# The attention layer of a four-layer latent backbone: another form of its scores, softmax division and value products

## The chip, the cores and the metric

The kernel runs on one core of a Trainium2 chip. The time is that of one launch in device microseconds; the median of several runs counts, and for the kernel before there are three: 2109.61, 2110.99 and 2111.64 us. The profile is that of one further execution.

## The reference

A block of four layers with mixers A, B, C, A, each followed by an MLP, on 256 latent and 256 context tokens of width 1024, in fp32. The change lies in mixer B, layer 1: attention of 16 query heads of 64 columns on 4 key heads, with a learned sink logit for each head. Latent queries see all context tokens and the latent tokens within 128 positions; context queries see context tokens alone.

```python
def sink_softmax(scores, sink):
    m = sink
    for s in scores:
        m = jnp.maximum(m, jnp.max(s, axis=-1))
    ps = [jnp.exp(s - m[..., None]) for s in scores]
    denom = jnp.exp(sink - m)
    for p in ps:
        denom = denom + jnp.sum(p, axis=-1)
    return [p / denom[..., None] for p in ps]

def swa_mixer(xc, xl, w_qkv, sinks, w_out, ang_row, ang_col, ctx_out):
    scale = B_HEAD_DIM ** -0.5
...
    mask = (jnp.abs(qpos - kpos) <= B_WINDOW) & (kpos >= 0) & (kpos < S)
    s_loc = jnp.einsum('bnqhgd,bnkhd->bnhgqk', qb, kb).astype(jnp.float32) * scale
    s_loc = jnp.where(mask[None, :, None, None], s_loc, -jnp.inf)
    s_ctx = jnp.einsum('bnqhgd,bchd->bnhgqc', qb, kc).astype(jnp.float32) * scale
    p_loc, p_ctx = sink_softmax([s_loc, s_ctx], sink[None, None, :, :, None])
    o_l = (jnp.einsum('bnhgqk,bnkhd->bnqhgd', p_loc.astype(vb.dtype), vb)
           + jnp.einsum('bnhgqc,bchd->bnqhgd', p_ctx.astype(vc.dtype), vc))
    yl = o_l.reshape(bn, S, D_MODEL) @ w_out
    if ctx_out:
        s_c = jnp.einsum('bqhgd,bkhd->bhgqk', qc, kc).astype(jnp.float32) * scale
        (p_c,) = sink_softmax([s_c], sink[None, :, :, None])
        o_c = jnp.einsum('bhgqk,bkhd->bqhgd', p_c.astype(vc.dtype), vc)
        yc = o_c.reshape(bn, xc.shape[1], D_MODEL) @ w_out
```

## The kernel before

Tokens lie along the free dimension: a tile `h[:, c, :]` holds 128 of the 1024 columns for 512 tokens, 0 to 255 latent and 256 to 511 context. Each weight block (128x1024 raw) is loaded by the queue of SP, cast to a high half on ScalarE (L241) and to the remaining low half on VectorE (L246). A product is the sum of three: high by high, high weight by low input, low weight by high input (`mm3`, L390 to L392). `w_get(ahead)` hands out the next block in a fixed list (`weight_order`) and has blocks split up to `ahead` further ones; four raw blocks and five pairs of halves are held.

The engines work off the instructions in the order in which the code issues them. So the order of calls in `mixer_b` is the schedule.

Mixer B first computes keys and ten blocks `u` of 128 columns (0 and 1 are keys, 2 to 9 queries), each with `chunk`: 24 products of 512 columns, after which `evac` splits the result into halves (`put`); the latent half is rotated first (`rotate`, and one TensorE product in `rest`). A query tile `Q2` holds the high half of one head's 64 columns on 64 partitions and the low half on the other 64, a key tile `K2` the high half of the keys on both. Then `v_step` computes values, and 32 units follow, a unit being 128 queries of two heads (`hh` 0 and 1) that share `G`, `blk` and `j`; `blk` 0 and 1 are latent queries on 512 keys, 2 and 3 context queries on 256. The order of blocks is 0, 2, 1, 3: four latent units, four context units, and so on, eight blocks in all. In step `x` of `attend`:

- `s1(x)` makes the scores of two heads in a bank each: one full-height product (high and low query halves by high keys, L1288), one of 64 rows for the low half of the keys (L1292), and for latent queries the window mask, added through an identity product of 256 columns (L1295).
- `s4(x-2)` transposes the exponentials (L1348), and ScalarE copies them out (L1350). `over_sum(x-2)` puts the reciprocal of each sum, as a diagonal matrix, through a product with ones (L1369), so that it lies in the layout of the result.
- `pv(x-3)` multiplies by the values, 128 query columns at a time (L1360).
- `s2(x)` takes on VectorE the maxima (L1309, L1314) and for unit `x-1` the sums' reciprocals and diagonals, and on ScalarE the exponentials with their sums (L1331).

After four units `block_end` multiplies the result by the reciprocals on VectorE (L1381); in the next step ScalarE casts it (L1338), and VectorE subtracts for the low half (L1339). The tile `h` is scratch during this and is saved to and restored from HBM. The output projection (`residual`, L565) follows: two of its eight blocks are begun among the last units, three follow as chunks, three go into `transition`, which also sums squares for the next normalisation (`stats_add`, L434) and takes their sum over partitions in a TensorE product (`stats_mm`, L465).

## Time and profile before

| | |
|---|---|
| median of three runs | 2110.99 us (2109.61 to 2111.64) |
| the profiled execution | 2114.74 us |
| its span on the core | 2113.0 us |
| TensorE busy | 2053.4 us (97%) |
| VectorE busy | 1453.5 us (69%) |
| ScalarE busy | 948.9 us (45%) |
| chain of waits, TensorE's share | 92% |

The span runs from the first instruction to the last; the launch takes somewhat longer. Shares are means over stages that differ. Matmuls are pipelined: the time from one start to the next tells their cost, not the length of a row.

### The profile page before, as it was taken

The page shows a single profiled execution, that of the slowest core. Times are in us where ns is not written, and L with a number is a line of the kernel's source. Part 1 is how long each engine was busy: PE and PEld are TensorE (multiplying, and loading weights), DVE is VectorE, ACT ScalarE, POOL GpSimd, SP SyncE. Part 2 cuts the span into 40 slices and gives each one's busy share as a digit, 9 for nine tenths or more (in the row PEclk, how much of TensorE's full clock was granted, in tenths as well). Part 3 has the DMA queues.
Part 4 walks back from the last instruction along what each step waited for, and adds up shares of the span by engine and source line. Part 5 has one row for each costly group of instructions (what it writes and reads, how often), then busy time and mean ns, then how long its engine had stood idle before and what let it go on. Part 6 is the DMA issues. An engine that isn't in the chain of part 4 may idle for free.

```text
span 2113.0 us, 30325 instructions
## 1 busy us (share of the span) xinstructions
PE 2053.4 (97%) x11730; PEld 1751.2 (83%) x11730; DVE 1453.5 (69%) x2652; ACT 948.9 (45%) x1814; POOL 87.0 (4%) x138
## 2 busy tenths in 40 slices
PE   6989999999999999999999999999999999989998
PEld 4767798888889878988888988898888899889997
DVE  5667777787777775677777764467777776576554
ACT  3436653324236685624333343262433435556554
POOL 0123100000000000000000000000000000310000
PEclk9999999999999999999999999999999999999999
DMA  9783245565553104266565433236556533635552
GB/s 300 272 264 103 64 135 179 177 193 185 184 170 119 50 2 138 92 189 189 179 194 175 130 112 98 94 108 189 187 180 197 179 122 104 175 103 180 184 185 91
DMA packets 97025, 326.11 MB, mean 154 GB/s; under 512 B 17760, under 2 KB 18928, under 8 KB 96240
## 3 DMA queue, kind: packets, MB, share of 16 engines
q1 hardware_dynamic: 81184, 293.81, 43.5%
q0 software_dynamic: 15152, 29.83, 4.6%
q8 instruction: 92, 1.51, 0.3%
q10 hardware_dynamic: 544, 0.52, 0.1%
q14 instruction: 53, 0.43, 0.1%
HBM read 319.73 MB, written 4.33 MB: 153 GB/s over the span
## 4 chain that ended last, share of the span: by engine, by line
PE 92%; DVE 3%; DMA 2%; ACT 2%; issue 1%; POOL 0%; SPq 0%; DVEq 0%; ACTq 0%
PE bank L390 25%; PE bank L392 25%; PE bank L391 25%; PE bank L591 2%; PE bank L592 2%; PE bank L594 2%; PE bank L422 1%; PE bank L1348 1%; PE bank L423 1%; PE bank L424 1%; PE bank L1360 1%; DMA ab<-dar 1%; PE bank L1288 1%; PE bank L1025 1%; DVE wlo L246 1%; PE bank L1000 1%
## 5 line engine op out<-in xcount | busy, mean ns | idle before, releaser
L390 PE MATMUL bank<-xh,whi 128*128 128x512 f32 (+1 forms) x1600 | 579.4, 362 | 1.7 <-ACT h L912 1.0
L241 ACT CAST whi<-raw 128x1024 fp32r<-128x1024 f32 x374 | 387.1, 1044 | 421.1 <-PE bank L391 382.8
L391 PE MATMUL bank<-xl,whi 128*128 128x512 f32 (+1 forms) x1600 | 574.4, 359 | 0.2
L392 PE MATMUL bank<-xh,wlo 128*128 128x512 f32 (+1 forms) x1600 | 573.9, 359 | 0.0
L246 DVE TENSOR_TENSOR wlo<-raw,whi 128x1024 fp32r<-128x1024 f32 x374 | 455.6, 1225 | 152.5 <-ACT whi L241 151.9
L353 DVE SCALAR_TENSOR_TENSOR junk<-ada,cbc 128x1024 bf16<-128x1024 f32 x320 | 390.7, 1221 | 18.1 <-DMA ada<-in_ada 13.8
L390 PE MATMUL bank<-hh,whi 128*128 128x512 f32 (+1 forms) x1096 | 384.5, 351 | 0.0
L392 PE MATMUL bank<-hh,wlo 128*128 128x512 f32 (+1 forms) x1096 | 383.9, 350 | 0.0
L391 PE MATMUL bank<-hl,whi 128*128 128x512 f32 (+1 forms) x1096 | 383.9, 350 | 0.0
L390 PEld LDWEIGHTS bank<-xh,whi 128*128 128x128 f32 x1600 | 304.9, 191 | 49.9 <-ACT h L912 1.6
L392 PEld LDWEIGHTS bank<-xh,wlo 128*128 128x128 f32 x1600 | 304.9, 191 | 44.3
L391 PEld LDWEIGHTS bank<-xl,whi 128*128 128x128 f32 x1600 | 305.0, 191 | 44.0 <-DVE xl L945 1.0
L391 PEld LDWEIGHTS bank<-hl,whi 128*128 128x128 f32 x1096 | 207.4, 189 | 27.4
L392 PEld LDWEIGHTS bank<-hh,wlo 128*128 128x128 f32 x1096 | 207.4, 189 | 27.2
L390 PEld LDWEIGHTS bank<-hh,whi 128*128 128x128 f32 x1096 | 207.4, 189 | 27.1
L565 DVE SCALAR_TENSOR_TENSOR h<-bank,mod,h 128x256 f32<-128x256 f32 x280 | 125.6, 479 | 133.1 <-PE bank L392 133.1
L676 DVE TENSOR_TENSOR hl<-q,hh 128x512 fp32r<-128x512 f32 (+1 forms) x137 | 81.5, 595 | 170.5 <-ACT q L675 170.2
L673 ACT ACTIVATE r<-bank 128x512 f32<-128x512 f32 (+1 forms) x137 | 70.8, 517 | 269.2 <-PE bank L392 266.2
L459 ACT ACTIVATE sq<-h 128x256 f32<-128x256 f32 (+1 forms) x74 | 36.0, 487 | 139.4 <-DVE h L565 114.2
L591 PE MATMUL bank<-xh,whi 128*128 128x256 f32 x312 | 81.4, 289 | 3.5 <-ACT xh L527 3.5
L592 PE MATMUL bank<-xh,wlo 128*128 128x256 f32 x312 | 80.2, 285 | 0.0
L674 ACT ACTIVATE hh<-r 128x512 fp32r<-128x512 f32 (+1 forms) x137 | 75.9, 554 | 4.6
(274 smaller groups left out, 2129.3 us busy)
## 6 DMA issues: line engine op xcount, KB each, us to landing
raw<-in_wts SPq DMA_DIRECT2D x374, 512.0 KB, 4.2
ada<-in_ada SPq DMA_DIRECT2D x160, 512.0 KB, 3.5
start<-in_ada SPq DMA_DIRECT2D x16, 512.0 KB, 9.1
first<-in_ada POOLq DMA_DIRECT2D x12, 512.0 KB, 6.0
cbc<-line POOLq DMA_DIRECT2D x4, 1024.0 KB, 7.8
rb<-dnm POOLq DMA_DIRECT2D x16, 256.0 KB, 7.1
ab<-dar POOLq DMA_DIRECT2D x16, 256.0 KB, 12.2
h<-in_hin SPq DMA_DIRECT2D x4, 512.0 KB, 6.8
```

Source lines behind the costliest of these rows:

```text
L241: self.nc.scalar.copy(hi, self.raw[j])
L246: self.nc.vector.tensor_tensor(out=lo, in0=self.raw.pop(j), in1=hi.bitcast(F32), op=ALU.subtract)
L353: nc.vector.scalar_tensor_tensor(out=junk, in0=w, scalar=1.0, in1=self.cbc[:, s, :], op0=ALU.mult, op1=ALU.mult, accum_out=self.mods[l][:, ...
L390: mm(out, lhsT=whi, rhs=xhi, start=first, stop=False)
L391: mm(out, lhsT=whi, rhs=xlo, start=False, stop=False)
L392: mm(out, lhsT=wlo, rhs=xhi, start=False, stop=last)
L565: self.nc.vector.scalar_tensor_tensor(out=self.h[:, m, a:b], in0=o[:, a - sl.start : b - sl.start], scalar=mod[:, gate + m, s : s + 1], in ...
L591: mm(o[:, :T], lhsT=w[0][:, c], rhs=hi[:, sl], start=(k == 0), stop=False)
L592: mm(o[:, :T], lhsT=w[1][:, c], rhs=hi[:, sl], start=False, stop=False)
L673: nc.scalar.activation(r[:, :n], o, AF.Relu)
L674: nc.scalar.activation(hh[:, sl], r[:, :n], AF.Square)
L676: nc.vector.tensor_tensor(out=hl[:, sl], in0=q[:, :n], in1=hh[:, sl].bitcast(F32), op=ALU.subtract)
```

## The change

The low half of the keys now fills both halves of its own tile for each key head (`KL[g]`), so its product takes the same 128-row query tile as the high half's; the mask product covers only the 128 columns that can be masked. `maxima` takes both heads of a unit in one VectorE instruction. The exponentials are multiplied by the reciprocal of their sum on VectorE before they are transposed (`normalise`), in place of the diagonal product and of the multiplication at the block's end. Two units (a pair `y`) go into one value product of 256 columns. Scores lie in banks 3, 4 and 6, 7, transposes in a ring of banks 0, 1, 2, results in bank 5; one in four of the copies of a latent pair is made on VectorE. The query blocks 8 and 9 come after the values (their weights too, in `weight_order`), the second of them among the first units, and five of the output projection's blocks are begun at the end; their second halves follow, each with the split of one weight block.

```diff
@@ weight_order
-            order += [("colq", "b_w_qkv", i, m) for m in range(8)]
+            order += [("colq", "b_w_qkv", i, m) for m in range(6)]
             order += [("mov", "b_w_qkv", i, 1280, 256, kk) for kk in range(2)]
+            order += [("colq", "b_w_qkv", i, m) for m in range(6, 8)]
@@ mixer_b
-            KL = [bp.tile([128, 512], F32R, name=f"KL{G}") for G in range(2)]
+            KL = [bp.tile([128, 512], F32R, name=f"KL{g}") for g in range(4)]
...
                     away = slice(64 - 64 * hh, 128 - 64 * hh)
                     if u < 2:
                         hi = K2[2 * u + hh]
-                        lo = KL[u][rows, sl]
+                        lo = KL[2 * u + hh]
                         nc.scalar.copy(hi[away, sl], src[rows])
+                        parts.append((rows, hi[rows, sl], lo[rows, sl]))
+                        parts.append((rows, hi[rows, sl], lo[away, sl]))
                     else:
                         hi = Q2[u - 2][hh]
-                        lo = hi[away, sl]
+                        parts.append((rows, hi[rows, sl], hi[away, sl]))
                     nc.scalar.activation(hi[rows, sl], src[rows], AF.Copy, scale=scale)
-                    parts.append((rows, hi[rows, sl], lo))
...
-                def rest():
-                    rp = self.aux()[:, 0:T]
+                def rest(bank=None):
+                    rp = (self.aux() if bank is None else bank)[:, 0:T]
...
-            for u in range(3, 10):
+            for u in range(3, 8):
             units = [(G, blk, j) for G in range(2) for blk in (0, 2, 1, 3) for j in range(4)]
...
+            N = len(units) // 2
+            bk = self.banks
+            tring, po = [bk[0], bk[1], bk[2]], bk[5]
+            S, P, sums = {}, {}, {}
...
-                ss = [ring[2 * (x % 2) + hh] for hh in range(2)]
+                at = 3 + 3 * (x % 2)
+                ss = self.allb[:, at : at + 2, 0:nk]
                 qs = Q2[G * 4 + j]
                 for hh in range(2):
-                    nc.tensor.matmul(ss[hh][:, :nk], lhsT=qs[hh][:, ts_], rhs=K2[2 * G + hh][:, k0:512], start=True, stop=False)
+                    g = 2 * G + hh
+                    nc.tensor.matmul(ss[:, hh, :], lhsT=qs[hh][:, ts_], rhs=K2[g][:, k0:512], start=True, stop=False)
+                    nc.tensor.matmul(ss[:, hh, :], lhsT=qs[hh][:, ts_], rhs=KL[g][:, k0:512], start=False, stop=not lat)
+                if lat:
+                    c = (1 - blk) * 128
+                    for hh in range(2):
+                        nc.tensor.matmul(
+                            ss[:, hh, c : c + 128], lhsT=self.ident16, rhs=self.mask_w[:, blk * T + c : blk * T + c + 128],
+                            start=False, stop=True,
+                        )
+                S[x] = ss
+            def maxima(x):
+                G, blk, j = units[x]
+                y, a = divmod(x, 2)
+                if a == 0:
+                    sums[y] = [bq.tile([128, 4], F32, tag=t, name=t, bufs=4) for t in ("ngm", "es", "rs")]
+                ngm = sums[y][0]
+                c = slice(2 * a, 2 * a + 2)
+                ci = G * 4 + j
+                nc.vector.tensor_reduce(ngm[:, c], S[x], axis=AX.X, op=ALU.max, negate=True)
+                nc.vector.tensor_tensor(out=ngm[:, c], in0=ngm[:, c], in1=self.nsinks[:, 2 * ci : 2 * ci + 2], op=ALU.min)
+                if a == 1:
+                    nc.vector.tensor_tensor(
+                        out=sums[y][1], in0=ngm, in1=self.nsinks[:, 2 * ci - 2 : 2 * ci + 2], op=ALU.subtract
+                    )
+            def exps(x):
+                y, a = divmod(x, 2)
+                ngm, es, rs = sums[y]
+                P[x] = []
                 for hh in range(2):
...
+                    p = bq.tile([128, 512], F32, tag="p", name="p", bufs=8)
+                    nk = S[x].shape[-1]
+                    at = 2 * a + hh
+                    nc.scalar.activation(
+                        p[:, :nk], S[x][:, hh, :], AF.Exp, bias=ngm[:, at : at + 1], accum_out=rs[:, at : at + 1]
+                    )
+                    P[x].append(p[:, :nk])
+                if a == 1:
+                    nc.scalar.activation(es, es, AF.Exp)
+            def normalise(y):
+                ngm, es, rs = sums.pop(y)
+                nc.vector.tensor_tensor(out=rs, in0=rs, in1=es, op=ALU.add)
+                nc.vector.reciprocal(rs, rs)
+                for a in range(2):
                     for hh in range(2):
...
+                        p = P[2 * y + a][hh]
+                        nc.vector.tensor_scalar(p, p, rs[:, 2 * a + hh : 2 * a + hh + 1], None, op0=ALU.mult)
+            def turn(x):
+                nk = len(keys_of(units[x][1])[0]) * 128
+                at = 2 * (x % 4)
+                ps = P.pop(x)
+                if nk == 512:
+                    for hh in range(2):
+                        tp = tring[tpos[0] % 3]
+                        tpos[0] += 1
+                        for c in range(0, nk, 128):
+                            nc.tensor.transpose(tp[:, c : c + 128], ps[hh][:, c : c + 128], self.ident)
+                        if hh * (x % 2):
+                            nc.vector.tensor_copy(self.h[:, at + hh, :], tp)
+                        else:
+                            nc.scalar.copy(self.h[:, at + hh, :], tp)
+                else:
+                    tp = tring[tpos[0] % 3].rearrange("p (a k) -> p a k", a=2)
+                    tpos[0] += 1
+                    for hh in range(2):
+                        for c in range(0, nk, 128):
+                            nc.tensor.transpose(tp[:, hh, c : c + 128], ps[hh][:, c : c + 128], self.ident)
+                    nc.scalar.copy(self.h[:, at : at + 2, 0:nk], tp)
+            def pv(y):
+                G, blk, j = units[2 * y]
-                js = slice(j * 128, j * 128 + 128)
+                at = 4 * (y % 2)
                 for c, kc in enumerate(kcs):
                     for hh in range(2):
                         g = 2 * G + hh
                         nc.tensor.matmul(
-                            po[64 * hh : 64 * hh + 64, js], lhsT=vv[:, kc, g * 64 : g * 64 + 64], rhs=PT[x][hh][:, c, :],
+                            po[64 * hh : 64 * hh + 64, j * 128 : j * 128 + 256], lhsT=vv[:, kc, g * 64 : g * 64 + 64],
+                            rhs=self.h[:, at + hh : at + hh + 3 : 2, c * 128 : c * 128 + 128],
                             start=(c == 0), stop=(c == len(kcs) - 1),
                         )
...
+            def block_end(y):
+                G, blk, _ = units[2 * y]
+                sl, cs = slice(blk * 128, blk * 128 + 128), slice(G * 4, G * 4 + 4)
+                t = po.rearrange("p (j t) -> p j t", j=4)
+                nc.scalar.copy(self.xh[:, cs, sl], t)
+                nc.vector.tensor_tensor(out=self.xl[:, cs, sl], in0=t, in1=self.xh[:, cs, sl].bitcast(F32), op=ALU.subtract)
+            early = []
+            def begin(o):
+                early.append((self.w_get(-1), o))
+                self.unit(o, early[-1][0], self.x_chunk, ALL, range(4))
+            def query(u, o, between, ahead):
+                w = self.w_get(ahead)
+                self.unit(o, w, self.x_chunk, ALL, range(4))
+                between()
+                self.unit(o, w, self.x_chunk, ALL, range(4, NK))
+                evac(u, o, ALL)
+            vo = [bk[j] for j in (5, 0, 1, 2)]
             for kk in range(2):
                 w = self.w_get(3 - kk)
                 for kx in range(4):
-                    self.v_step(w, 4 * kk + kx, outs, 256)
+                    self.v_step(w, 4 * kk + kx, vo, 256)
                     if pend and kx in (0, 2):
                         pend.pop(0)()
                     if kk == 1 and kx % 2 == 1:
                         s1(kx // 2)
             for tcn in range(4):
-                nc.scalar.copy(vv[:, tcn, :], outs[tcn][:, 0:256])
+                nc.scalar.copy(vv[:, tcn, :], vo[tcn][:, 0:256])
             for x in range(2):
...
+                maxima(x)
+                exps(x)
+            query(8, bk[5], lambda: None, 2)
+            for y in range(1, N + 3):
+                if y >= 5 and y % 2 == 1:
+                    block_end(y - 4)
+                t = 2 * (y - 2)
+                if 2 <= y < N + 2:
+                    turn(t)
+                if y < N:
+                    s1(2 * y)
+                    maxima(2 * y)
+                if y <= N:
+                    normalise(y - 1)
+                if y == 1:
+                    query(9, bk[1], lambda: pend.pop(0)(bk[0]), 3)
+                if y == 2:
+                    pend.pop(0)(bk[2])
+                if y in (N, N + 1):
+                    begin(bk[3 + 3 * (y - N)])
+                if 2 <= y < N + 2:
+                    turn(t + 1)
+                if y < N:
+                    exps(2 * y)
+                    s1(2 * y + 1)
+                    maxima(2 * y + 1)
+                    exps(2 * y + 1)
+                if y in (N, N + 1):
+                    begin(bk[4 + 3 * (y - N)])
+                if y >= 3:
+                    pv(y - 3)
+                if y in (N - 3, N - 1):
                     self.wsplit_to(self.wsplit + 1)
...
+                if y > N:
+                    c = slice(4 * (y - N - 1), 4 * (y - N - 1) + 4)
+                    nc.gpsimd.dma_start(out=self.h[:, c, :], in_=saved[:, c, :])
+            begin(bk[0])
+            block_end(N - 1)
         res = self.residual(l, 16, 512)
         for m, (w, o) in enumerate(early):
             self.unit(o, w, self.x_chunk, ALL, range(4, NK))
             res(m, o, ALL)
-        for m in range(2, 5):
-            self.chunk(m, self.x_chunk, ALL, res)
+            self.wsplit_to(self.wpos + 1 + m)
+        self.bpos = 1
         yield self.x_chunk, res, (5, 6, 7)
```

The lists of three engines show what moved. The first is TensorE in the loop, context units whose predecessors have latent queries, before the change: scores (`K`, `KL` are key halves, `Q` query tiles), transposes (`cons`), diagonal products and the value product (`h`, `vv`) of one step.

```order
L1288 MATMUL bank<-K_5009,Q_5454 128x256
L1288 MATMUL bank<-K_5010,Q_5455 128x256
L1292 MATMUL bank<-KL_5013,Q_5454 128x256
L1292 MATMUL bank<-KL_5013,Q_5455 128x256
L1348 MATMUL bank<-cons,p 128x128 x8
L1369 MATMUL bank<-diag,ones 64x128 x2
L1360 MATMUL bank<-h,vv 64x128 x8
```

And one pass of the new loop at the same kind of place:

```order
L1355 MATMUL bank<-cons,p 128x128 x8
L1292 MATMUL bank<-K_5009,Q_5462 128x256
L1293 MATMUL bank<-KL_5013,Q_5462 128x256
L1292 MATMUL bank<-K_5010,Q_5463 128x256
L1293 MATMUL bank<-KL_5014,Q_5463 128x256
L1355 MATMUL bank<-cons,p 128x128 x8
L1292 MATMUL bank<-K_5009,Q_5464 128x256
L1293 MATMUL bank<-KL_5013,Q_5464 128x256
L1292 MATMUL bank<-K_5010,Q_5465 128x256
L1293 MATMUL bank<-KL_5014,Q_5465 128x256
L1375 MATMUL bank<-h,vv 64x256 x8
```

The scores of a pair's two units lie on either side of the second unit's transposes, and the value product closes the pass for two units. VectorE before, at a block's end: the multiplication `on`, one step's maxima, sums and diagonals, the low half `xl`.

```order
L1381 TENSOR_TENSOR on<-bank,on 128x512
L1309 TENSOR_REDUCE ngm<-bank 128x1
L1312 TENSOR_TENSOR rs<-rs,es 128x2
L1314 TENSOR_REDUCE ngm<-bank 128x1
L1316 RECIPROCAL rs<-rs 128x2
L1318 TENSOR_TENSOR ngm<-ngm,nsinks 128x2
L1321 TENSOR_SCALAR diag<-cons,rs 128x128
L1323 TENSOR_TENSOR es<-ngm,nsinks 128x2
L1325 TENSOR_SCALAR diag<-cons,rs 128x128
L1339 TENSOR_TENSOR xl<-on,xh 128x4x128
```

VectorE in the change, the same place: the division of the pair before (`p`), a copy, the maxima of a pass's second unit, and the low half at the head of the next pass.

```order
L1338 TENSOR_TENSOR rs<-rs,es 128x4
L1339 RECIPROCAL rs<-rs 128x4
L1343 TENSOR_SCALAR p<-p,rs 128x512 x4
L1357 COPY h<-bank 128x512
L1313 TENSOR_REDUCE ngm<-bank 128x2
L1314 TENSOR_TENSOR ngm<-ngm,nsinks 128x2
L1316 TENSOR_TENSOR es<-ngm,nsinks 128x4
L1386 TENSOR_TENSOR xl<-bank,xh 128x4x128
L1313 TENSOR_REDUCE ngm<-bank 128x2
```

The division now stands between a pass's two maxima, and the low half ahead of the next pass's first. ScalarE before, a block's end in a latent step:

```order
L1331 ACTIVATE p,rs<-bank,ngm 128x512 x2
L1335 ACTIVATE es<-es 128x2
L1338 CAST xh<-on 128x4x128
L1350 COPY h<-bank 128x512 x2
L1331 ACTIVATE p,rs<-bank,ngm 128x256 x2
```

ScalarE in the change, with a block's end between two context passes:

```order
L1333 ACTIVATE es<-es 128x4
L1359 COPY h<-bank 128x512 x3
L1328 ACTIVATE p,rs<-bank,ngm 128x256 x4
L1333 ACTIVATE es<-es 128x4
L1385 CAST xh<-bank 128x4x128
L1359 COPY h<-bank 128x512 x3
```

The cast now reads the value product's bank itself; it stands behind the exponentials of both units of the pass and ahead of the next pass's copies.

## Rows read from the trace of the kernel before

**Rows 1.** Windows, mixer B's stretch and an early one: time, busy time by engine, granted clock.

```profile
719.78:838.64 118.86, 117.99 (x980) 87.80 (x979) 79.88 (x286) 85.25 (x253) 2.65 (x5) 1.00 0.16 55
20.00:53.00 33.00, 30.90 (x158) 19.89 (x158) 18.30 (x44) 11.76 (x21) 2.17 (x3) 0.90 0.92 286
```

**Rows 2.** Timeline of TensorE in the loop: start, length in us, line, operation.

```profile
746.97 0.73 PE L1288 MATMUL bank<-K,Q 128*128 128x512 f32 x2
...
748.29 1.04 PE L1348 MATMUL bank<-cons,p 128*128 128x128 f32 x8
749.26 0.44 PE L1369 MATMUL bank<-diag,ones 128*64 128x128 f32 x4
749.53 1.04 PE L1360 MATMUL bank<-h,vv 128*64 128x128 f32 x16
750.50 0.51 PE L1288 MATMUL bank<-K,Q 128*128 128x256 f32 x2
...
773.20 0.51 PE L1288 MATMUL bank<-K,Q 128*128 128x256 f32 x2
```

**Rows 3.** Timeline of TensorE in a query projection, two starts.

```profile
665.92 0.39 PE L391 MATMUL bank<-xl,whi 128*128 128x512 f32 x1
666.15 0.39 PE L392 MATMUL bank<-xh,wlo 128*128 128x512 f32 x1
```

**Rows 4.** Timeline of VectorE and TensorE around the transition into the MLP.

```profile
833.40 0.88 DVE L565 SCALAR_TENSOR_TENSOR h<-bank,mod,h 128x256 f32<-128x256 f32 x2 [1.12 <-PE bank L392]
...
835.99 1.23 DVE L246 TENSOR_TENSOR wlo<-raw,whi 128x1024 fp32r<-128x1024 f32 x1 [0.25 <-ACT whi L241]
...
848.51 0.42 DVE L434 TENSOR_TENSOR ssum<-ssum,sq 128x256 f32<-128x256 f32 x1 [0.54 <-ACT sq L459]
...
849.08 0.61 PE L465 MATMUL bank<-ssum,ones 128*128 128x256 f32 x2
```

**Rows 5.** Timeline of ScalarE and VectorE in the loop, context step, then latent steps.

```profile
730.57 0.50 ACT L1331 ACTIVATE p<-bank,ngm 128x256 f32<-128x256 f32 x1
...
731.48 0.23 ACT L1335 ACTIVATE es<-es 128x2 f32<-128x2 f32 x1
...
739.40 0.61 ACT L1338 CAST xh<-on 128x512 fp32r<-128x512 f32 x1
740.04 0.69 DVE L1339 TENSOR_TENSOR xl<-on,xh 128x512 fp32r<-128x512 f32 x1 [1.29 <-ACT xh L1338]
740.65 0.68 DVE L1309 TENSOR_REDUCE ngm<-bank 128x1 f32<-128x512 f32 x1
741.25 0.15 DVE L1312 TENSOR_TENSOR rs<-rs,es 128x2 f32<-128x2 f32 x1
...
742.04 0.16 DVE L1318 TENSOR_TENSOR ngm<-ngm,nsinks 128x2 f32<-128x2 f32 x1
...
742.30 0.69 ACT L1331 ACTIVATE p<-bank,ngm 128x512 f32<-128x512 f32 x1 [1.35 <-DVE ngm L1318]
...
743.64 0.20 ACT L1335 ACTIVATE es<-es 128x2 f32<-128x2 f32 x1
...
743.87 0.16 DVE L1312 TENSOR_TENSOR rs<-rs,es 128x2 f32<-128x2 f32 x1 [0.55 <-ACT es L1335]
```

**Rows 6.** VectorE's groups by form: line, operation, shapes, count; busy, mean ns, idle before.

```profile
L565 DVE SCALAR_TENSOR_TENSOR h<-bank,mod,h 128x256 f32<-128x256 f32 x280 | 125.6, 479 | 133.1 <-PE bank L392 133.1
...
L1321 DVE TENSOR_SCALAR diag<-cons,rs 128x128 f32<-128x128 f32 x32 | 9.0, 281 | 0.0
...
L495 DVE SCALAR_TENSOR_TENSOR rs_a<-rs_a,rs_x 128x256 f32<-128x256 f32 x14 | 6.0, 426 | 1.6
...
L914 DVE TENSOR_SCALAR h<-h 128x512 f32<-128x512 f32 x8 | 3.3, 418 | 0.0
...
L914 DVE TENSOR_SCALAR h<-h 128x256 f32<-128x256 f32 x8 | 2.3, 284 | 0.0
```

**Rows 7.** The page's costliest groups, the cast of weights.

```profile
L241 ACT CAST whi<-raw 128x1024 fp32r<-128x1024 f32 x374 | 387.1, 1044 | 421.1 <-PE bank L391 382.8
```

More of the change, by code (lines that the diff above doesn't have):

```diff
@@ L1341, in s4 @@
-            def s4(x):
-                G, blk, j = units[x]
-                nkc = len(keys_of(blk)[0])
-                PT[x] = []
-                for hh in range(2):
-                    tp = outs[hh].rearrange("p (c t) -> p c t", c=4)
-                    for c in range(nkc):
-                        nc.tensor.transpose(tp[:, c, :], P[x][hh][:, c * 128 : c * 128 + 128], self.ident)
-                    t = self.h[:, 2 * (x % 4) + hh, :].rearrange("p (c t) -> p c t", c=4)
-                    nc.scalar.copy(t[:, :nkc, :], tp[:, :nkc, :])
-                    PT[x].append(t)
@@ L1353, in pv @@
-            def pv(x):
-                G, blk, j = units[x]
+                    g = 2 * G + hh
[8 more added lines that the diff above has]
+                        )
@@ L1360, in pv @@
                         nc.tensor.matmul(
-                            po[64 * hh : 64 * hh + 64, js], lhsT=vv[:, kc, g * 64 : g * 64 + 64], rhs=PT[x][hh][:, c, :],
+                            po[64 * hh : 64 * hh + 64, j * 128 : j * 128 + 256], lhsT=vv[:, kc, g * 64 : g * 64 + 64],
+                            rhs=self.h[:, at + hh : at + hh + 3 : 2, c * 128 : c * 128 + 128],
                             start=(c == 0), stop=(c == len(kcs) - 1),
                         )
-            def over_sum(x):
-                j = units[x][2]
-                for hh in range(2):
-                    nc.tensor.matmul(
-                        pr[64 * hh : 64 * hh + 64, j * 128 : j * 128 + 128], lhsT=self.ones[:, 0:64], rhs=diag[x][hh],
-                        start=True, stop=True,
-                    )
-                if j == 3:
-                    t = bq.tile([128, 512], F32, tag="on", name="on", bufs=2)
-                    nc.scalar.copy(t, pr)
-                    over.append(t)
@@ L1378, in block_end @@
-            def block_end(G, blk):
-                sl = slice(blk * 128, blk * 128 + 128)
-                t = over.pop()
-                nc.vector.tensor_tensor(out=t, in0=po, in1=t, op=ALU.mult)
-                cs = slice(G * 4, G * 4 + 4)
-                block_done.append((self.xh[:, cs, sl], self.xl[:, cs, sl], t.rearrange("p (j t) -> p j t", j=4)))
-            N = len(units)
-            over, block_done, early = [], [], []
-            def attend(x):
-                if x >= 7 and x % 4 == 3:
-                    block_end(*units[x - 4][:2])
-                if x < N:
-                    s1(x)
-                if 2 <= x < N + 2:
-                    s4(x - 2)
-                    over_sum(x - 2)
-                if 3 <= x < N + 3:
-                    pv(x - 3)
-                s2(x)
+            def block_end(y):
[4 more added lines that the diff above has]
+                nc.vector.tensor_tensor(out=self.xl[:, cs, sl], in0=t, in1=self.xh[:, cs, sl].bitcast(F32), op=ALU.subtract)
@@ new lines, in mixer_b @@
+            early = []
[9 more added lines that the diff above has]
+            vo = [bk[j] for j in (5, 0, 1, 2)]
+            assert self.bpos % 6 == 5
```

61 lines of the change are left out of this document (1 added, 60 removed).

## The prediction

> **What bounds the kernel now.** I read the windows view first. From the end of the value projection (719.78 us) to the transition into the MLP (838.64 us), mixer B's stretch, TensorE is busy 117.99 of 118.86 us, VectorE 79.88, ScalarE 85.25 [rows 1]: the stretch ends when TensorE has worked off its list. Then TensorE's timeline in the loop over units: eight units (four of latent queries, four of context queries) go from 750.50 to 773.20, 22.7 us, without a gap. In a latent unit the scores take 1.32 us (746.97 to 748.29), eight transposes 0.97, the diagonal products 0.27, the value product 0.97 [rows 2]. Last come the timeline of VectorE and ScalarE and VectorE's groups by form, for the durations of what the change puts on these two.
>
> I call a pass of the new loop y, its two units A and B, and a pair of units L (latent queries) or C (context queries); pairs come L L C C, so four passes make a cycle, to be set against 22.7 us.
>
> **TensorE's own work.** An L unit's scores become four full-height products of 512 columns, 0.23 each as in the projections [rows 3], and two masks of 128 columns, a quarter of that: 1.03 in all. C has half the columns and no mask: 0.48. Transposes stay, 0.97 for eight, about 0.55 for four. The diagonal products go. The value product of two units streams the same columns with half the starts: not over 2 x 0.97 = 1.94, hardly under 1.7; I take 1.82, and 0.97 for C. A cycle is 4 x (1.03 + 0.97 + 0.48 + 0.55) + 2 x (1.82 + 0.97) = 17.7 us, 5.0 less than 22.7. Over four cycles that is 20 us, if TensorE still sets the pace.
>
> **What VectorE gets.** One maximum over both heads covers 1024 elements: 1.22, as the 128x1024 row of 1.23 [rows 4] and 512 elements at 0.68 [rows 5] say. The division runs over the exponentials themselves, 128x512 four times per L pair. No row has this form. A tensor_scalar with a constant takes 418 ns for 512 columns and 284 for 256; a factor per partition adds 53 ns (479 against 426); the 128x128 row with such a factor takes 281, near 284 - 67 + 53 = 270 and far from the 350 of one element per cycle [rows 6]. So 0.47, and since the next instruction starts 0.08 before the end (740.65 + 0.68 against 741.25 [rows 5]), 0.39 each, 0.26 for C; the other end is 0.65 and 0.40. The sum of weights, its reciprocal and their waits are 0.37 ahead. A division takes 0.37 + 4 x 0.39 = 1.93 (L) or 1.41 (C).
>
> The Trainium skill (VectorE: DVE Perf Modes, section The perf-mode tier table) gives fp32 tensor_scalar between SBUF tiles twice the rate of tensor_tensor; our 418 ns rows agree, and this lowers the chance of the slow end below.
>
> **The chain that replaces TensorE.** VectorE's list in a pass is: maxima A, division of the pair before, a copy of transposed weights (when the pair being turned is L), maxima B. ScalarE's is: copies, exponentials A, exponentials B. At a block's end ScalarE casts the result behind exponentials B, and VectorE's subtraction waits for that cast at the head of the next pass; behind it are queued maxima A and with them all else. Lengths [rows 5]: maxima to the exponentials' start 1.22 + 0.03 + 0.16 + 0.10 = 1.51 (L), 0.98 (C); exponentials of a unit 1.34 (742.30 to 743.64), C 0.91 (730.57 to 731.48); sink exponential 0.20, after it 0.03 until VectorE; cast 0.61, then 0.03; subtraction 0.61 until the next may start. A cycle from one maxima B to the same four passes on:
> 1. L, maxima B to maxima A over the block end: 1.51 + 1.34 + 0.10 + 0.61 + 0.03 + 0.61 = 4.20
> 2. maxima A (1.34) and division L: 3.27
> 3. maxima B to the division, which waits for the sink exponential: 1.51 + 1.34 + 0.20 + 0.03 = 3.08
> 4. division L and a copy (0.60): 2.53
> 5. C, over the block end: 0.98 + 0.91 + 0.10 + 0.61 + 0.03 + 0.61 = 3.24
> 6. maxima A (0.81), division C, copy: 2.82
> 7. maxima B (0.99), maxima A of L (1.34), division C: 3.74
> Sum 22.9 us. In step 5 to 7 TensorE is later still: an L pair needs four transpose banks and has three, so the last four transposes wait for ScalarE's first copy, which stands behind exponentials B and the cast; scores B, the value product and the next pass's scores A are queued behind them. From maxima B: 0.98 + 0.91 + 0.10 + 0.48 + 0.60 + 0.12 = 3.2 until they start, then 0.5 + 0.48 + 1.82 + 0.55 + 1.03 + 0.2 = 4.6, 7.8 against 7.05 on VectorE: 0.7 more. A cycle takes 23.6 us, 0.9 more than before, with TensorE waiting for 5.9 of it.
>
> **The ends.** Time 0 is the end of the value projection. Two projection blocks of queries (24 products, 5.46 each) and two rotations (0.9 together) now lie behind it, so before's 118.9 becomes 118.9 + 10.9 + 0.9 = 130.7 us up to the transition. These blocks bring VectorE three low halves of weights (1.15 each) and the queries' own splitting and rotation, ten instructions at 0.34 to 0.43, and the maxima of unit 3 are queued behind them: from 7.4 us (first block 6.5, ScalarE 0.9) on 0.7 + 1.34 + 1.93 + 2.3 + 2.4 + 1.0 = 9.6, so they start at 17.0, while TensorE is through with scores at 14.5. From there to pass 4's maxima B it is steps 3 to 7 and the 0.7, 16.1, less 2.3 for the block end that isn't there yet, plus 2.4 for the last query's rotation: 33.2. Two cycles: 80.4. Steps 1 and 2: 87.9 (pass 13). There a weight block is split: VectorE's low half waits behind exponentials B and ScalarE's cast of 1.04 [rows 7], and maxima A behind it: 1.51 + 1.34 + 0.10 + 1.04 + 0.03 + 1.15 + 0.81 + 1.93 + 0.60 = 8.5, then 6.0 to the end of that pass's value product as above: 102.4. From there TensorE has enough to do: four turns 2.2, five half blocks 13.65, value products 3.8, five second halves 13.65: 135.7. In the second halves VectorE needs 3.74 for each (833.40 to 835.99, and 1.15 [rows 4]) against TensorE's 2.73. It ends at 21.6, and three evacuations of about 1.4 bring it to 25.8; the product over the sums of squares comes at 13.65 + 3 x 2.88 + 1.8 = 24.1. Before, the last addition ended just ahead of it (848.51 + 0.42 against 849.08 [rows 4]), so now about 1.8 are lost. Sum 137.5, against 130.7: **6.8 us slower**.
>
> **Costed at nothing.** The keys' second copy of the low half is eight more 256-column VectorE instructions, 2.7 us, in the transition ahead of the mixer; the query blocks behind cover them, and uncovered they cost 2.7. The order of weights changes no transfer's size, and raw tiles are asked for four ahead. The saved stream comes back in two transfers instead of four, with five half blocks of TensorE work beside them; a late one costs under 2 us.
>
> The profiled execution took 2114.74 us around a span of 2113.0; on it the sum gives 2121.5. It lay 3.75 us above the runs' median of 2110.99, on which I forecast 2118 us. What the measurement can't tell from no change is 0.2%, about 4.2 us.
>
> **Rivals.**
> - Faster: TensorE sets the pace. It needs the loop maxima, exponentials, scores to hide inside 17.7 us. For it: VectorE's bare work in a cycle is about 18.4 us by the same rows, ScalarE's less. Against it: both lists are in order, and steps 1, 3 and 5 hold 4.6 us in which VectorE waits for ScalarE. The stage would lose about 20 us and keep 4 or 5 for the ends: 2096. The point from which it decides is a cycle of 21.7 us (6.8 over some 3.6 cycles off 23.6). Chance 0.17.
> - No change: the cycle is 22.9, and the split in pass 13 (2.9), the lag in the second halves (1.8) and some of the fill are hidden: 6 to 7 us less, 2111. For it: TensorE has a reserve of half blocks there. Chance 0.21.
> - Division at one element per cycle: 4 x 0.26 more per L pair and 4 x 0.14 per C pair, 3.2 per cycle, 11 in all: 2129. For it: no row shows 512 columns with a factor per partition. Against it: the 281 ns row. Chance 0.08.
> - The chain as laid out: 0.54.
>
> The Trainium skill (TensorE: Matmul & The Clock Gate, section Why this matters for your kernels) warns that idle gaps put TensorE back to the lower of its clocks. Here the granted clock was 0.90 in a stretch that follows idle time, 1.00 in mixer B [rows 1]. By that rule the new gaps of up to 2.5 us in the fill could slow a few us of matmuls, some 5 us more (2123, inside the range), to which I give 0.04 within the chain's chance.
>
> The chain's own range is 2112 to 2125. The whole range reaches down into the faster rival and up to the slow division: 2103 to 2130. Slower by over 0.2%: 0.08 and most of the chain's 0.54, 0.59. Within: 0.23. Faster: 0.18.
>
> **What would show it.** TensorE's busy share of the loop near 75% with its waits on VectorE and ScalarE; eight units in 23 to 24 us; the subtraction of the block's end waiting about 2 us for its cast; maxima B right behind the division; the division at 0.47 us. Wrong if TensorE is gapless in the loop, if eight units take under 21.7 us, or if the division shows 0.7 us.

## The result and the profile after

The changed kernel takes 2124.81 us (median of 2123.55 to 2126.57) against 2111.22 of the kernel before: ratio 1.0064, 95% interval 1.0051 to 1.0076, 13.6 us slower. Its profiled execution took 2125.98 us.

First the windows view of the changed kernel: time, busy time of TensorE, its weight loads, VectorE, ScalarE and GpSimd, the granted clock, DMA. The first row is four passes of the loop, the second four us within them, the third the first passes.

```profile
750.80:774.90 24.10, 20.01 (x136) 14.09 (x136) 18.28 (x49) 15.97 (x49) 0.00 (x0) 0.93 0.00 1
...
756.00:760.00 4.00, 4.00 (x22) 2.74 (x21) 2.54 (x7) 2.76 (x12) 0.00 (x0) 0.57 0.02 4
...
722.00:737.00 15.00, 9.08 (x49) 7.48 (x48) 11.69 (x32) 10.42 (x31) 0.00 (x0) 0.77 0.19 64
```

Where TensorE was gapless at full clock [rows 1], it is now busy for 20.0 of 24.1 us, part of that near the lower of the clock's two levels (1.2 and 2.4 GHz): 0.57 of full speed in the second row. Eight units took 22.7 us [rows 2] and take 24.1. The timeline of TensorE shows the largest wait of a cycle and what stands behind it:

```profile
752.23 0.60 PE L1355 MATMUL bank<-cons,p 128*128 128x128 f32 x4
755.43 0.66 PE L1355 MATMUL bank<-cons,p 128*128 128x128 f32 x4 [2.60 <-ACT h L1359]
...
756.49 1.93 PE L1375 MATMUL bank<-h,vv 128*64 128x256 f32 x8
758.35 1.86 PE L1355 MATMUL bank<-cons,p 128*128 128x128 f32 x8
```

The last four transposes of a latent pair wait for the bank that ScalarE's copy gives free. VectorE's timeline over one cycle of the chain, the counterpart of [rows 5]:

```profile
768.47 1.22 DVE L1313 TENSOR_REDUCE ngm<-bank 128x2 f32<-128x1024 f32 x1
...
772.02 0.69 DVE L1386 TENSOR_TENSOR xl<-bank,xh 128x512 fp32r<-128x512 f32 x1 [1.95 <-ACT xh L1385]
772.63 1.22 DVE L1313 TENSOR_REDUCE ngm<-bank 128x2 f32<-128x1024 f32 x1
...
774.36 1.67 DVE L1343 TENSOR_SCALAR p<-p,rs 128x512 f32<-128x512 f32 x4
775.95 1.22 DVE L1313 TENSOR_REDUCE ngm<-bank 128x2 f32<-128x1024 f32 x1
...
779.03 0.16 DVE L1338 TENSOR_TENSOR rs<-rs,es 128x4 f32<-128x4 f32 x1 [0.67 <-ACT es L1333]
...
781.64 0.68 DVE L1313 TENSOR_REDUCE ngm<-bank 128x2 f32<-128x512 f32 x1
...
784.23 0.69 DVE L1386 TENSOR_TENSOR xl<-bank,xh 128x512 fp32r<-128x512 f32 x1 [1.52 <-ACT xh L1385]
784.84 0.68 DVE L1313 TENSOR_REDUCE ngm<-bank 128x2 f32<-128x512 f32 x1
...
787.69 0.68 DVE L1313 TENSOR_REDUCE ngm<-bank 128x2 f32<-128x512 f32 x1
...
789.72 1.23 DVE L1313 TENSOR_REDUCE ngm<-bank 128x2 f32<-128x1024 f32 x1 [0.95 <-ACT p L1328]
...
792.52 1.22 DVE L1313 TENSOR_REDUCE ngm<-bank 128x2 f32<-128x1024 f32 x1
```

The subtraction at the head of a pass waits 1.95 us for its cast, and the maxima behind it wait with it.

In the table, "stage" is the time in the profile from the first copy of the values to the product over the sums of squares. Where queries 8 and 9 lie inside it, their 11.8 us (10.9 and 0.9) are taken off. "Cycle" is four passes, from one block end's subtraction to the next but one. The stage leaves out one source of scatter that the whole time has: seven of the kernels are the same up to the values, yet in their profiles these copies begin between 702.6 and 706.4 us. Each stage and cycle is read from one execution, so how far a stage repeats is not shown.

| kernel | ratio to before, interval | stage | cycle |
|---|---|---|---|
| before | 1 | 130.2 | 22.7 |
| changed | 1.0064 (1.0051 to 1.0076) | 141.8 | 24.1 |
| e1_low_later | 1.0034 (1.0021 to 1.0047) | 137.8 | 22.5, 23.0 |
| e2_copy_first | 1.0074 (1.0058 to 1.0091) | 145.9 | 25.5 |
| e3_both | 1.0022 (1.0013 to 1.0031) | 134.7 | 21.1 |
| e4_gap_filled | 1.0054 (1.0039 to 1.0069) | 142.5 | 23.8 |
| e5_queries_back | 1.0042 (1.0027 to 1.0057) | 138.9 | 24.0 |
| e6_scores_in_before | 0.9978 (0.9968 to 0.9987) | 126.4 | 21.8 |
| e7_order | 0.9997 (0.9988 to 1.0007) | 128.3 | 20.3 |
| e8_order_qback | 0.9979 (0.9970 to 0.9988) | 125.0 | 20.3 |
| e9_division_short | 1.0021 (1.0012 to 1.0031) | 134.9 | 22.7, 21.8 |
| e11_order_three_qback | 0.9974 (0.9964 to 0.9984) | 124.6 | 20.3 |
| e12_scores_ahead | 0.9991 (0.9982 to 1.0000) | 128.2 | 20.7 |
| e13_act_copies | 0.9964 (0.9951 to 0.9978) | 122.6 | 19.3 |

### The profile page after: what moved, and what is told of

Same layout as the page of the kernel before. It is cut to its first block, busy times and chain, and to the rows that moved or that the text cites. A ratio compares the mean times of both kernels' runs of the same rounds, so it can differ in the third digit from the quotient of the medians.

```text
span 2124.2 us, 29594 instructions
## 1 busy us (share of the span) xinstructions
PE 2043.5 (96%) x11410; PEld 1741.8 (82%) x11410; DVE 1461.3 (69%) x2580; ACT 937.3 (44%) x1766; POOL 84.7 (4%) x136
## 4 chain that ended last, share of the span: by engine, by line
PE 57%; DVE 1%; ACT 1%; issue 0%; DMA 0%; POOL 0%; DVEq 0%; ACTq 0%
PE bank L391 17%; PE bank L392 17%; PE bank L393 17%; PE bank L592 1%; PE bank L593 1%; PE bank L595 1%; PE bank L423 1%; PE bank L424 1%; PE bank L425 1%; DMA ab<-dar 0%; DVE wlo L247 0%; PE bank L1001 0%; PE bank L466 0%; ACT rb L960 0%; PE bank L1026 0%
## 5 line engine op out<-in xcount | busy, mean ns | idle before, releaser
L566 DVE SCALAR_TENSOR_TENSOR h<-bank,mod,h 128x256 f32<-128x256 f32 x280 | 125.5, 479 | 128.2 <-PE bank L393 128.0
```

Of the source, the lines that this page charges most:

```text
L566: self.nc.vector.scalar_tensor_tensor(out=self.h[:, m, a:b], in0=o[:, a - sl.start : b - sl.start], scalar=mod[:, gate + m, s : s + 1], in ...
```

## The experiments

**The order in VectorE's queue.** In the changed kernel, the subtraction for the low half behind the first maxima of the pass (2119.24 us):

```diff
-                nc.vector.tensor_tensor(out=self.xl[:, cs, sl], ... op=ALU.subtract)
+                def low(): ...   # the same instruction
...
                     maxima(2 * y)
+                    if low:
+                        low()
```

> The changed kernel (2124.8 us), with the block end's subtraction on VectorE issued behind the first maxima of the pass instead of ahead of them; every instruction is kept. Theory A (the in-order queues of VectorE and ScalarE set the pace): at a block end between latent passes the first maxima no longer wait for ScalarE's cast (1.94 us of waiting at 747.92), and the whole chain behind is about 1.6 us earlier, three times; at the ends between context passes TensorE's scores come late anyway, so nothing: 4 to 5 us in all, 2120. Rival B (VectorE's and TensorE's amount of work sets the pace): the same instructions, no change, 2124 to 2126.

5.6 us less with the same instructions: theory A, and a little more than its 4 to 5, against B. The subtraction waits 0.33 us in the first block end where it waited 1.94, and a cycle is 1.0 to 1.6 us shorter. VectorE's row in this run:

```profile
744.60 0.69 DVE L1387 TENSOR_TENSOR xl<-bank,xh 128x512 fp32r<-128x512 f32 x1 [0.33 <-ACT xh L1385]
```

**The third bank.** VectorE's copy on the first transposed tile (2127.55 us):

```diff
-                        if hh * (x % 2):
+                        if x % 2 == 0 and hh == 0:
```

> The changed kernel, with VectorE's copy of a latent pair made on the first of its four transposed tiles instead of the last; ScalarE makes the other three, so the count is kept. Theory A: TensorE's wait of 2.60 us for its third bank (755.43, 779.53) becomes about 1.3, since VectorE copies in a gap in which it waits for exponentials; one pass in four gets 0.6 us shorter on VectorE and TensorE's scores two passes later are earlier: 1.2 to 1.7 us per cycle, 5 to 7 us in all, 2118 to 2120, and the granted clock of 0.57 behind that wait is gone or shorter. Rival B (amount of work): 2124 to 2126.

Both were wrong: it is no faster. The median is 2.7 us higher, which the intervals of the two ratios don't tell from no change, but the stage is 4.1 us longer and the cycle 1.4. TensorE's timeline in that kernel:

```profile
751.49 0.65 PE L1355 MATMUL bank<-cons,p 128*128 128x128 f32 x4 [1.29 <-DVE h L1357]
...
758.25 1.12 PE L1355 MATMUL bank<-cons,p 128*128 128x128 f32 x4 [2.56 <-DVE h L1357]
```

The wait fell to 1.29 as expected, but one pass on, at a block end, the copy now stands behind the subtraction that waits for its cast, and 2.56 us arise there. With both edits (2116.72 us) nothing stands ahead of it:

> The changed kernel with both edits of the two runs before: VectorE copies the first transposed tile of a latent pair, and the block end's subtraction stands behind the first maxima. Alone the early copy cost 2.7 us, since at block ends it was queued behind the subtraction and TensorE waited 2.56 us there instead of in the pass before; alone the later subtraction gained 5.6. Theory A (order in the queues): now nothing stands in front of the copy, TensorE's wait of 2.4 us for its third bank falls to 1.3 or less in both context passes, the cycle goes from 22.5 to about 21.3, 4 to 5 us below the later subtraction alone: 2114 to 2116. Rival B (the copy only moves the wait): 2119 to 2122.

The cycle is 21.1 us and the stage 3.1 shorter than with the later subtraction alone; of the time 2.5 us, somewhat short of what A expected. The two edits do not add: the third-bank edit lengthens the stage by itself and shortens it once the subtraction has moved.

**Another order of the pass.** On top of both edits: each unit's scores ahead of the transposes, the first unit's exponentials with them, the division behind both maxima (2110.44 us):

```diff
+                if y < N:
+                    s1(2 * y)
                 if 2 <= y < N + 2:
                     turn(t)
                 if y < N:
-                    s1(2 * y)
                     maxima(2 * y)
...
+                if y < N:
+                    exps(2 * y)
+                    s1(2 * y + 1)
...
+                if 2 <= y < N + 2:
+                    turn(t + 1)
+                if y < N:
+                    maxima(2 * y + 1)
                 if y <= N:
                     normalise(y - 1)
...
-                if 2 <= y < N + 2:
-                    turn(t + 1)
                 if y < N:
-                    exps(2 * y)
-                    s1(2 * y + 1)
-                    maxima(2 * y + 1)
                     exps(2 * y + 1)
```

> The same, with the pass in another order: scores of a unit before the transposes of the pair before, and the division behind both maxima instead of between them, so that VectorE never waits in a pass for the exponentials of the pass just begun. No instruction is added or taken away. Theory A (in-order queues): the loop falls to what the engines need, about 18.3 us per cycle on VectorE and on TensorE, say 19 to 20 instead of 24: 16 to 20 us less than the changed kernel, 2105 to 2109. Rival B (VectorE is full: its bare work is the pace): at most what its waits were, to 2115; rival D: the division now comes too late for the transposes and TensorE waits for it, 2120.

A again: 14.4 us less than the changed kernel, with not an instruction more or less, a little under the 16 expected; 6.3 of them come on top of the two edits. The cycle is 20.3 us, and the granted clock in it 1.00:

```profile
742.73:763.02 20.29, 18.62 (x139) 13.21 (x138) 18.17 (x50) 16.04 (x48) 0.00 (x0) 1.00 0.01 1
```

VectorE's busy time in a cycle is as in the changed kernel (18.17 and 18.28): its work was never the 24.1 us, the waits in its queue were. But the loop, 2.4 us per cycle faster than before's, only brings the time back to before's; the rest sits at the ends.

**The division's amount.** In the changed kernel, only 64 columns of each tile divided; the rest of the division is left out (2116.07 us):

```diff
-                        nc.vector.tensor_scalar(p, p, rs[...], None, op0=ALU.mult)
+                        nc.vector.tensor_scalar(p[:, 0:64], p[:, 0:64], rs[...], None, op0=ALU.mult)
```

> The changed kernel with the division done on the first 64 columns of each tile of exponentials alone (the others stay undivided, which leaves out part of the computation): instruction counts and order are kept, VectorE does about 0.96 us less per latent and 0.44 per context pair. Theory A (VectorE's list sets the pace nearly all the time): 1.9 to 2.8 us per cycle, 8 to 11 in all, 2114 to 2117. Rival F (TensorE's or ScalarE's path sets it): under 3 us, 2122 to 2125.

8.7 us less, in A's range, with 1.4 to 2.3 us per cycle. VectorE is busy 2.4 to 2.6 us less per cycle (15.9 and 15.7 for 18.3), so most of that is time: the division does lie on the path, beside the order of the queue.

**The clock.** TensorE given products of its own in the gap (2123.83 us):

```diff
+                        if x % 8 == 1 and hh and x > 8:
+                            fill(x // 2 + 2)   # 22 products of 256 columns, bf16
                         for c in range(0, nk, 128):
                             nc.tensor.transpose(...)
```

> The changed kernel, with 22 products of 256 columns (bf16, about 0.11 us each, 2.4 us) put on TensorE ahead of the transposes that wait 2.60 us for a bank, in three passes; they write columns of the result bank that the next value product begins anew, so no result changes. Theory C (the clock that falls behind this wait costs time on the path): the granted clock stays at 1.00 behind the wait, the value product of 8 takes 0.97 instead of 1.86 us and the eight transposes 0.9 instead of 1.6, the wait of VectorE for scores (0.95 to 0.99 us) goes away: 0.9 us less per cycle, 2122, though TensorE does more. Rival D (the clock is off the path): no gain, 2125 to 2126.

```profile
751.51 2.56 PE L1348 MATMUL bank<-mask_w,ident 128*128 128x256 bf16 x22
754.26 0.65 PE L1363 MATMUL bank<-cons,p 128*128 128x128 f32 x4 [0.18 <-ACT h L1367]
...
755.31 1.08 PE L1383 MATMUL bank<-h,vv 128*64 128x256 f32 x8
756.33 1.09 PE L1363 MATMUL bank<-cons,p 128*128 128x128 f32 x8
...
759.46 0.66 PE L1363 MATMUL bank<-cons,p 128*128 128x128 f32 x4 [1.13 <-ACT h L1367]
```

The clock stays at 1.00 behind the gap and the two groups take 1.08 and 1.09 instead of 1.93 and 1.86. Yet the cycle loses only 0.2 to 0.3 us, not the 0.9 of C: the 1.13 us wait for the next copy, 759.46, takes the gain. From the last of the loop's subtractions to the sums of squares it takes 1.3 us longer, and the time is unchanged within its interval. 2123.83 lies between what C and D expected; the cycle decides. So the fallen clock is real and nearly off the path, D rather than C.

**The ends.** Queries 8 and 9 ahead of the values again (2120.67 us):

```diff
-            order += [("colq", "b_w_qkv", i, m) for m in range(6)]
+            order += [("colq", "b_w_qkv", i, m) for m in range(8)]
...
-            for u in range(3, 8):
+            for u in range(3, 10):
...
-            query(8, bk[5], lambda: None, 2)
...
-                    query(9, bk[1], lambda: pend.pop(0)(bk[0]), 3)
```

> The changed kernel with query blocks 8 and 9 (and their weights) again ahead of the values; the loop is untouched. By the chain (theory A) these blocks behind the values cover little: the loop's first passes wait for VectorE, which has the blocks' own splits and rotations to do as well. From the values' end to the fifth pass's second maxima there are 37.1 us, of which 11.8 are the two blocks; without them the chain alone needs 1.3 + 22.8 = 24.1: 1.2 us less, 2123 to 2124. Rival E (the blocks fill TensorE's idle time in the first passes, as intended): without them 5 us or more later, 2130.

4.1 us less in time, 2.9 in the stage: the direction of A, more than its 1.2. With the other order of the pass as well (2106.41 us):

> The pass in the other order (2110.4 us), and query blocks 8 and 9 again ahead of the values, which alone took 4.1 us from the changed kernel. Theory A (these blocks bring VectorE more than they give TensorE, whatever the order of the loop): again about 4 us, 2106. Rival E (with the loop's waits gone, VectorE no longer holds the first passes up, and the blocks cover TensorE's idle time): no gain or a loss, 2110 to 2114.

Again 4.0 us less. Three begun blocks instead of five on top (2105.56 us):

```diff
-            begin(bk[0])
...
-        self.bpos = 1
+        self.bpos = 0
+        for m in range(3, 5):
+            self.chunk(m, self.x_chunk, ALL, res)
```

> The run beside it, with three blocks of the output projection begun among the last passes instead of five and the other two done whole behind them. Theory A (VectorE needs 3.74 us for each second half and TensorE 2.73, so the sums of squares are late and TensorE waits 1.44 us for them): with two whole blocks of 5.46 us at the end VectorE catches up, the wait goes, 1.5 us less than the run beside it: 2104 to 2105. Rival G (the fourth and fifth block cover waits for the last exponentials and copies): TensorE waits 1 to 3 us there, 2106 to 2109.

The wait for the sums of squares is gone, but TensorE waits 0.9 us for the last cast and subtraction instead, and VectorE 3.6 for the saved tile; 0.4 us shorter in the stage, nothing that the time can tell. Between A and G.

**Beyond.** On top of the run before, the scores of the next pass's first unit ahead of the value product (2109.94 us):

```diff
+                if y < N - 1:
+                    s1(2 * y + 2)
                 if y >= 3:
                     pv(y - 3)
```

> The same with three begun blocks, and the scores of each pass's first unit issued ahead of the value product of the pass before. In the other order of the pass VectorE still waited 0.9 and 0.4 us for scores behind the value product of 1.9 us, in each latent pass. Theory A: these waits go, the cycle falls from 20.3 to about 19.2, 4 us below the three begun blocks alone: 2100 to 2101. Rival B (VectorE full: the waits come back elsewhere): 2103 to 2105.

Slower than both expected, and 4.4 us slower than the run before (3.6 in the stage). Two rows, TensorE and then VectorE:

```profile
748.58 0.39 PE L1293 MATMUL bank<-K,Q 128*128 128x256 f32 x1 [0.73 <-ACT p L1329]
```

```profile
758.33 1.23 DVE L1314 TENSOR_REDUCE ngm<-bank 128x2 f32<-128x1024 f32 x1 [1.23 <-PE bank L1299]
```

The early scores wait for the exponentials that still read their bank, and the wait of the first maxima has become one of the second. The last run has the other order of the pass, the queries ahead, five begun blocks, and no copy on VectorE (2104.24 us):

```diff
-                        if hh * (x % 2):
-                            nc.vector.tensor_copy(self.h[:, at + hh, :], tp)
-                        else:
-                            nc.scalar.copy(self.h[:, at + hh, :], tp)
+                        nc.scalar.copy(self.h[:, at + hh, :], tp)
```

> The pass in the other order, queries 8 and 9 ahead of the values (2106.4 us), five begun blocks, and all copies of transposed tiles on ScalarE, so that VectorE makes none (0.6 us less in two passes of four). In that kernel a cycle takes 20.3 us, of which VectorE is busy about 18.5 and TensorE 18.8; TensorE waits there for the division (0.6 and 0.3 us) and the subtraction (0.2 and 0.7), both late on VectorE. Theory B' (VectorE's amount of work is now the pace): the cycle falls to about 19.4, 3 us less in all, 2103. Rival A' (order again: with the first copy on ScalarE behind other work the third bank comes free late): TensorE waits 1 us or more in the context passes, 2106 to 2110.

```profile
742.96:762.25 19.29, 18.48 (x140) 13.14 (x138) 16.99 (x47) 16.93 (x50) 0.00 (x0) 1.00 0.01 1
```

B' was right to 0.1 us of the cycle, but not in that VectorE's work is the pace: it is busy 17.0 of 19.3 us and waits 1.10 and 0.42 for scores, while TensorE is busy 18.5. It is 0.36% faster than before (0.22 to 0.49%), the best of all, and 20.6 us below the changed kernel.

**One part alone in the kernel before.** The keys' low half over all 128 rows and the narrower masks; two small pools are a size smaller to make room (2108.07 us):

```diff
...
-                    rows = slice(64 * hh, 64 * hh + 64)
-                    nc.tensor.matmul(ss[hh][:, :nk], lhsT=qs[hh][rows, ts_], rhs=KL[G][rows, k0:512], ...)
+                    nc.tensor.matmul(ss[hh][:, :nk], lhsT=qs[hh][:, ts_], rhs=KL[g][:, k0:512], ...)
...
-                            s[:, 0:T], lhsT=self.ident16, rhs=self.mask_w[:, blk * T : blk * T + T], ...
+                            s[:, c : c + 128], lhsT=self.ident16, rhs=self.mask_w[:, blk * T + c : blk * T + c + 128], ...
```

> The kernel before (2111.2 us) with one part of the change alone: the keys' low half over all 128 rows, and masks of 128 columns; two small pools are one size smaller to make room. TensorE is gapless there, so what its scores lose is lost from the time. Theory A: by the changed kernel's starts a latent unit's scores take 1.14 to 1.24 us instead of 1.32 and a context unit's 0.55 instead of 0.75: 16 x 0.13 + 16 x 0.2 = 5 us, 2106. By the prediction's own figures (1.03 and 0.48 instead of 1.32 and 0.75): 9 us, 2102. Rival B: VectorE's eight more instructions for the keys (2.7 us) or the waits behind fewer TensorE cycles take it back: 2111.

Between A and B: 3.8 us less, 0.85 per cycle. A latent unit's scores take 1.16 us there (745.04 to 746.20) and a context unit's 0.59, so the prediction's 1.03 and 0.48 were too low. Where TensorE was the bound, its saved time was time.

```profile
745.04 0.50 PE L1290 MATMUL bank<-K,Q 128*128 128x512 f32 x1
...
746.20 1.04 PE L1349 MATMUL bank<-cons,p 128*128 128x128 f32 x8
...
748.41 0.39 PE L1290 MATMUL bank<-K,Q 128*128 128x256 f32 x1
...
749.00 1.04 PE L1349 MATMUL bank<-cons,p 128*128 128x128 f32 x8
```

## Why the prediction was right, and where its size was off

The forecast was slower by 7 us, by the chain through the in-order queues of VectorE and ScalarE; it is slower by 13.6, and e1, e3 and e7 show that chain as the cause: the same instructions in another order give the time back. The direction and the path were right, the size about half. Its milestones, from the end of the value projection (707.27), against rows of the changed kernel, VectorE's and then TensorE's:

```profile
725.68 1.23 DVE L1313 TENSOR_REDUCE ngm<-bank 128x2 f32<-128x1024 f32 x1
...
744.37 1.22 DVE L1313 TENSOR_REDUCE ngm<-bank 128x2 f32<-128x1024 f32 x1
...
800.00 1.22 DVE L1313 TENSOR_REDUCE ngm<-bank 128x2 f32<-128x1024 f32 x1
```

```profile
814.59 0.66 PE L1365 MATMUL bank<-cons,p 128*128 128x128 f32 x4
...
847.91 0.28 PE L391 MATMUL bank<-xh,whi 128*128 128x256 f32 x1
...
859.95 0.70 PE L466 MATMUL bank<-ssum,ones 128*128 128x256 f32 x2 [1.44 <-DVE ssum L435]
```

| milestone | predicted | measured |
|---|---|---|
| maxima of unit 3 | 17.0 | 18.4 |
| second maxima of pass 4 | 33.2 | 37.1 |
| two cycles on | 80.4 | 85.2 |
| second maxima of pass 13 | 87.9 | 92.7 |
| end of the next pass's value product | 102.4 | 107.3 |
| end of the five second halves | 135.7 | 140.6 |
| wait for the sums of squares | 1.8 | 1.4 |

- **The division** was taken as 0.47 us and takes 482 ns for 512 columns, 350 for 256; the rival of one element per cycle falls.

```profile
L1343 DVE TENSOR_SCALAR p<-p,rs 128x512 f32<-128x512 f32 x32 | 13.4, 482 | 0.3
...
L1343 DVE TENSOR_SCALAR p<-p,rs 128x256 f32<-128x256 f32 x32 | 9.1, 350 | 0.3
L1386 DVE TENSOR_TENSOR xl<-bank,xh 128x512 fp32r<-128x512 f32 x8 | 5.5, 692 | 21.5 <-ACT xh L1385 21.5
```

- **The cycle**, 23.6, is 24.1 (768.47 to 792.52). Steps 1 to 6 measure 4.16, 3.32, 3.08, 2.61, 3.20 and 2.85 against 4.20, 3.27, 3.08, 2.53, 3.24 and 2.82. Step 7 with TensorE's lateness takes 4.83 instead of 4.44: that is most of the difference. TensorE's busy share of a cycle is 83% and not the 75% of the prediction's sign, since at the lower clock the same products take longer.
- **The step that failed is the fill**, 33.2 for 37.1. Its first half is 1.4 late: VectorE's list starts 0.4 later (715.11, after ScalarE's copies) and waits 0.6 for ScalarE ahead of the last query halves. The second half took 18.7 for 16.2, and most of that is one term: "less 2.3 for the block end that isn't there yet".

```profile
733.85 0.68 DVE L1313 TENSOR_REDUCE ngm<-bank 128x2 f32<-128x512 f32 x1
...
741.57 1.22 DVE L1313 TENSOR_REDUCE ngm<-bank 128x2 f32<-128x1024 f32 x1 [2.09 <-PE bank L1365]
```

```profile
735.83 1.55 ACT L1359 COPY h<-bank 128x512 f32<-128x512 f32 x3
```

```profile
736.46 0.66 PE L1355 MATMUL bank<-cons,p 128*128 128x128 f32 x4 [0.17 <-ACT h L1359]
```

From the second maxima of the first of two context passes to the first maxima of the latent pass behind them it takes 8.08 us with a block end (781.64 to 789.72) and 7.72 without one (733.85 to 741.57): the missing block end saved 0.4 us, not 2.3. The prediction took it off VectorE's list, 7.05 + 0.7 - 2.3 = 5.5. What is left without it is the other path that the prediction names, TensorE's of 7.8, less the cast of 0.48, which is 7.3: the last four transposes wait for the third bank, hence for ScalarE's first copy behind the exponentials, and the next pass's scores stand behind them; VectorE waits 2.09 us for these.

The clock fell here too, 0.77 in the mean from 722 to 737. But the copy at 735.83 follows exponentials of the maxima at 733.85, which VectorE reached by its own list, and from 736 to 740 the granted clock is 0.99. By these rows the slow stretch lies off the path; no run took it away there. That the two query blocks behind the values cost 3 to 4 us is shown by e5 and e8.

- **From pass 13 on** the sum holds: 47.8 predicted from 87.9 to 135.7, 47.9 measured; the split's cost in pass 13 is as laid out.
- 142.1 instead of 137.5 makes +11.4 against 130.7 in the profile. The medians differ by 2 us more, since before's profiled execution lay 3.5 us above the median of its runs and the changed kernel's 1.2; where in the kernel those us lie is not shown.
- **The clock-gate rule** was to cost 5 us with a chance of 0.04. The gaps of 2.60 us did put the clock down, to 0.57 over the four us behind them in a cycle. The Trainium skill (TensorE: Matmul & The Clock Gate, section Why this matters for your kernels) warns of that. The price in the loop is 0.2 to 0.3 us per cycle by e4, and in the fill none by the rows above.
- **TensorE sets the pace** failed for the named reason: VectorE waiting for ScalarE. TensorE's work in a cycle was given as 17.7 and is 18.5 at full clock (e13). With the waits ordered away, e13's cycle lies under the 21.7 that the rival needed, and the kernel is faster than before.

## What to carry to other kernels

Work taken from the bounding engine is worth time only while the engines that receive it keep ahead; lay their in-order lists out as a chain, and look first at an instruction that waits at the head of a pass with others queued behind it. Where two paths meet, a term taken off one of them saves only what the other leaves: the block end that was missing in the fill was worth 0.4 us and not 2.3. Reorder before giving up on the amount: the same instructions took 24.1 or 20.3 us per cycle. Moving one waiting instruction can put the wait into the next queue (e2, e12), so test such edits together as well as apart.

## What was not expected

The scatter of 3.8 us in the start of the values' copies is as large as several of the effects studied. It arises early: of four of these kernels, TensorE had done 391 to 395 products by 100 us, but 885 to 912 by 200, and the one with 885 begins its copies last, the one with 912 first. And TensorE near half its clock for some 3 us in each cycle, 1.5 us more busy time (20.0 against 18.5 in e13), cost the cycle 0.2 to 0.3.
